# Routing searches started within the projection, first-product fill moved to later heads, one mask instruction, and both norms rearranged in a float32 block on one core

## The chip, the cores and the metric

The kernel runs on one core of a Trainium2 chip. The metric is the device time of one execution in microseconds (us). The core has TensorE (matmuls and transposes), VectorE (DVE), ScalarE (ACT), GpSimd (POOL) and SyncE (SP, which only issues transfers). Each engine works through its own instructions in a fixed order and waits on semaphores for the others.

## What is computed

One layer over 512 tokens of 1024 features, all in float32. The reference, cut to what matters:

```
xn = rms_norm(x, ln_mix_g)
proj = xn @ w_in
a_out = gmlp_spatial_gating(proj[..., :a0], proj[..., a0:a1], ...)
b_out = banded_chunk_attention(proj[..., q0:k0], proj[..., k0:v0], proj[..., v0:], ...)
x = x + concatenate([a_out, b_out]) @ w_out
x = x + peer_ffn(rms_norm(x, ln_ffn_g), w_query, sub_keys, expert_u, expert_v)
```

`rms_norm(x, g)` is `x * rsqrt(mean(x*x) + eps) * g`. `peer_ffn` routes each token: for each of 8 heads a query of two halves of 128 is projected, each half is scored against 128 sub-keys, the 16 best of each half are kept, their 256 sums are searched for the best 16 pairs, and a softmax over those gives gates to 16 of 16384 experts:

```
q = (xb @ w_query).reshape(tokens, HEADS, 2, 128)
sc = einsum('thpd,hpkd->thpk', q, sub_keys)
s_top, i_top = top_k(sc, 16)
best, pos = top_k(s_top[:, :, 0, :, None] + s_top[:, :, 1, None, :], 16)
eidx = i_top0 * 128 + i_top1 at pos
out = sum over (head, k) of softmax(best) * gelu(xb . u[eidx]) * v[eidx]
```

## The kernel before, in words

**Splitting.** Each float32 operand of a large product is split into a high and a low part, and `mm3` (lines 150 to 154) makes three matmuls of them: high x high, high x low, low x high. `load_split` (121 to 133) loads a weight tile of 128 x 1024 into `raw` (three buffers), makes `hi` on ScalarE (line 129) and `lo` on VectorE or GpSimd (line 130); `hi` and `lo` have five buffers each.

**Order.** The text order of the program and priorities give each engine its order through a scheduler, except inside a `manual_schedule` block, where the named engines keep the written order. `issue_after(i)` puts what it encloses behind instruction `i` on the engine of `i`; instructions of other engines are not bound by it.

**Opening (229 to 255).** Tokens stand in four tiles of 128. `norm_transposed` (164 to 186) takes each: ScalarE squares and sums (line 170), VectorE and ScalarE make the reciprocal root (159 to 161), VectorE multiplies by it and by the gain row, which was loaded to all partitions (173), TensorE transposes (178), ScalarE and VectorE make the high and low halves `xh` and `xl` (182, 183). Then the queries and keys are projected, token tile by token tile (253), and with the second half of their weights for all tiles (254).

**Attention and gating (282 to 442)** follow, not touched but for the row scale below.

**Second norm (455 to 478).** The output projection's residual sums (line 464) are made for token tiles in the order 1, 2, 3, 0, and each tile goes through `norm_transposed`, to `xbh` and `xbl`. `behind_norm` holds the last two instructions of tile 3, and the splits and activations of the first two expert tiles (722 to 724) and the first query weights (676) are queued behind it. These first products need tokens 128 to 447 alone, so not tile 0.

**Routing (671 to 755).** TensorE makes, head by head, the two halves of the query (685), copied to `qt` by ScalarE (688), then the scores (696), copied out by ScalarE (699, 700). VectorE finds the best 16 of each of three token tiles and two halves (`best_keys`, `top16`, 595 to 610). For the head before, `pairs` (612 to 635) makes 50 candidate sums and `choose` (637 to 658) picks 16 of them: searches, six instructions that take one bit each of the 16 positions (646), and six predicated copies down a tree of values (656). Gathers of expert rows for 64 tokens go on GpSimd (518) with their dot products on VectorE (527), six a head from head 2 on.

As the route leaves TensorE free, first products of the dense expert layer are put in between: `first_products` (584 to 591), one tile of 128 experts by 320 tokens each, split on GpSimd, activated on ScalarE (581). `FILL` gives their number per head, and eight more, the bridge, follow the last head. Lines 750 and 751 copy `xbh` and `xbl` for the later stage, on GpSimd.

**One-hot stage (850 to 914).** Gates of all experts are made from one-hot products (819) of two factors, `bm` (GpSimd, 803) and `am` (VectorE, 811), stored and reloaded; the rest of the first products run in between. **Second products (1022 to 1034)** with the values follow, TensorE without a stop, while GpSimd gathers the rows of token tile 0.

## Time and profile before

| | us |
|---|---|
| median of 3 runs | 1438.88 (1437.36 to 1449.58) |
| the profiled execution | 1439.61 |
| its span, first to last instruction | 1437.8 |
| TensorE busy | 1387.7 |
| VectorE busy | 1157.9 |
| GpSimd busy | 701.0 |
| ScalarE busy | 610.7 |

The granted TensorE clock averages 0.994 over the span. In the lines of a timeline, the first number is the start in us, the second the duration in us, then come the engine (PE, DVE, ACT, POOL, SP), the line, the operation, what it writes and reads, its shapes and the count, and in brackets how long the engine stood idle before it and what ended that. In the table of stretches come the sum of time, then each engine's busy time and its instructions, the granted clock, the transfer engines' share and GB/s. A matmul's duration overlaps its neighbour's; the distance between two starts is its price in a row of them.

### The profile page before, as it was taken

The numbers are of one execution on the slowest core, as the hardware profiler recorded it, in microseconds if no ns is written. First come the engines' busy times: TensorE is split into PE (matmuls) and PEld (weight loads), VectorE is DVE, ScalarE is ACT, GpSimd is POOL, SyncE is SP. The second block draws the span as 40 slices with busy tenths as digits, with TensorE's granted clock in tenths as the row PEclk, the third lists the DMA queues.
The fourth block names the chain that finished last, engine by engine and source line by source line (L and its number), as shares of the span: only waits on it lengthen the run. The fifth ranks groups of instructions, "written<-read, shape, count | busy, mean of one in ns | idle before, by whom it ended". The sixth has DMA issues, their size and how long they took to land.

```text
span 1437.8 us, 21717 instructions
## 1 busy us (share of the span) xinstructions
PE 1387.7 (97%) x7808; PEld 1226.3 (85%) x7808; DVE 1157.9 (81%) x2548; ACT 610.7 (42%) x974; POOL 701.0 (49%) x479
## 2 busy tenths in 40 slices
...
GB/s 190 118 189 75 89 99 195 101 272 303 214 223 206 313 327 268 282 259 350 279 361 358 332 351 355 354 385 363 396 337 355 366 325 352 276 327 348 344 327 72
DMA packets 164315, 396.77 MB, mean 276 GB/s; under 512 B 12736, under 2 KB 75088, under 8 KB 162160
## 3 DMA queue, kind: packets, MB, share of 16 engines
...
q14 instruction: 46, 0.38, 0.1%
...
## 4 chain that ended last, share of the span: by engine, by line
PE 77%; DVE 12%; DMA 5%; ACT 3%; issue 2%; POOL 1%; SPq 0%; ACTq 0%; POOLq 0%; DVEq 0%
PE pa L1008 22%; PE px L1008 11%; PE pu L152 9%; PE pu L154 9%; PE pu L153 9%; PE pa L152 4%; PE pa L153 4%; PE pa L154 4%; PE pa L819 3%; DMA gd<-gst 2%; DVE lo L130 2%; POOL bm L803 1%; DVE acc L960 1%; DVE tree L656 1%; DVE rowe L527 1%
## 5 line engine op out<-in xcount | busy, mean ns | idle before, releaser
L129 ACT ACTIVATE hi<-raw 128x1024 fp32r<-128x1024 f32 x300 | 316.7, 1059 | 447.9 <-DMA raw<-in_vd 133.1
L130 DVE TENSOR_TENSOR lo<-raw,hi 128x1024 fp32r<-128x1024 f32 x247 | 310.3, 1257 | 90.1 <-ACT hi L129 89.0
L947 POOL DMA_INDIRECT row<-in_ud,eint x128 | 196.0, 1531 | 176.0 <-DVE acc L960 109.3
L958 POOL DMA_INDIRECT row<-in_vd,eint x128 | 185.2, 1447 | 173.6 <-DVE row L949 120.2
L152 PE MATMUL pu<-xch,hi 128*128 128x320 f32 x784 | 246.8, 315 | 3.1 <-ACT act L581 3.1
L153 PE MATMUL pu<-xcl,hi 128*128 128x320 f32 x784 | 242.0, 309 | 0.0
L154 PE MATMUL pu<-xch,lo 128*128 128x320 f32 x784 | 241.6, 308 | 0.0
L1008 PE MATMUL pa<-hi,wh 128*128 128x512 f32 x512 | 199.8, 390 | 0.0
L1008 PE MATMUL pa<-lo,wh 128*128 128x512 f32 x512 | 199.3, 389 | 0.0
L960 DVE SCALAR_TENSOR_TENSOR acc<-row,hw,acc 128x1024 f32<-128x1024 f32 x128 | 164.8, 1287 | 0.9 <-DMA row<-in_vd,eint 0.5
L130 POOL TENSOR_TENSOR lo<-raw,hi 128x1024 fp32r<-128x1024 f32 x53 | 126.9, 2408 | 69.3 <-ACT hi L129 68.5
L949 DVE SCALAR_TENSOR_TENSOR row<-row,xb 128x1024 f32<-128x1024 f32 x128 | 157.4, 1232 | 1.5 <-DMA row<-in_ud,eint 1.5
L1008 PE MATMUL pa<-hi,wl 128*128 128x512 f32 x512 | 158.3, 389 | 0.0
L152 PEld LDWEIGHTS pu<-xch,hi 128*128 128x128 f32 x784 | 147.7, 188 | 6.5 <-ACT act L581 5.0
L153 PEld LDWEIGHTS pu<-xcl,hi 128*128 128x128 f32 x784 | 147.7, 188 | 1.4
L154 PEld LDWEIGHTS pu<-xch,lo 128*128 128x128 f32 x784 | 147.6, 188 | 0.0
L819 PE MATMUL pa<-bm,am 128*128 128x128 f32 x768 | 98.5, 281 | 16.7 <-DVE am L811 6.4
L1008 PEld LDWEIGHTS pa<-hi,wl 128*128 128x128 f32 x512 | 96.1, 188 | 20.4
L1008 PEld LDWEIGHTS pa<-hi,wh 128*128 128x128 f32 x512 | 96.1, 188 | 20.3
L1008 PEld LDWEIGHTS pa<-lo,wh 128*128 128x128 f32 x512 | 96.1, 188 | 20.2
L819 PEld LDWEIGHTS pa<-bm,am 128*128 128x128 f32 x768 | 92.9, 195 | 21.5 <-POOL bm L803 7.5
L1008 PE MATMUL px<-hi,wh 128*128 128x512 f32 x256 | 100.5, 393 | 3.2 <-ACT hi L129 3.2
(224 smaller groups left out, 2633.6 us busy)
## 6 DMA issues: line engine op xcount, KB each, us to landing
raw<-in_uT SPq DMA_DIRECT2D x128, 512.0 KB, 5.7
raw<-in_vd SPq DMA_DIRECT2D x128, 512.0 KB, 6.1
...
gc<-gd SPq DMA_DIRECT2D x15, 256.0 KB, 10.8
```

What stands on the lines that cost most here:

```text
L129: nc.scalar.activation(hi, raw, AF.Copy)
L130: ins = eng.tensor_tensor(lo, raw, hi.bitcast(F32), op=ALU.subtract)
L152: nc.tensor.matmul(ps, lh[0], rh[0], start=first, stop=False)
L153: nc.tensor.matmul(ps, lh[0], rh[1], start=False, stop=False)
L154: nc.tensor.matmul(ps, lh[1], rh[0], start=False, stop=last)
L527: nc.vector.scalar_tensor_tensor(row, row, 1.0, xbu, op0=ALU.mult, op1=ALU.mult, accum_out=du[:, j:j + 1])
L819: nc.tensor.matmul(ps[:, i * P:(i + 1) * P], am[:, 4 * q + i, :], bm[:, 4 * q + i, :], start=True, stop=True)
L947: nc.gpsimd.indirect_dma_start(out=row, out_offset=None, in_=ud, in_offset=bass.IndirectOffsetOnAxis(ap=eint[:, j:j + 1], axis=0))
L949: nc.vector.scalar_tensor_tensor(row, row, 1.0, xb0, op0=ALU.mult, op1=ALU.mult, accum_out=hw[:, j:j + 1])
L958: nc.gpsimd.indirect_dma_start(out=row, out_offset=None, in_=vd, in_offset=bass.IndirectOffsetOnAxis(ap=eint[:, j:j + 1], axis=0))
L960: nc.vector.scalar_tensor_tensor(acc0, row, hw[:, j:j + 1], acc0, op0=ALU.mult, op1=ALU.add)
L1008: nc.tensor.matmul(accs[t][half], (wh, wh, wl)[k][:, b, tok], w[b][k % 2][:, ds_], start=first and k == 0, stop=last and k == 2)
```

## The change

The first norm: raw x is transposed and multiplied by the gain per feature (the gain now lies on partitions, 4 KB instead of a broadcast of 512 KB), and 1/rms is put in after the products, as the scale of the copies out of PSUM; the gated part takes it as a row (`rrow`), made by four transposes. The opening's order on TensorE, VectorE, ScalarE and SyncE is written out by hand, the first weights are loaded and split in pieces, and TensorE multiplies a tile of ones (8 products ahead of the first transposes, 5 behind them).

The second norm: the second expert tile's split waits for the scaling of the last tile in order (tile 0), the activations and the first query weights for that tile's halves; GpSimd's two copies come behind its splits of head 4.

The routing: the scores of a query's first half are made in the middle of the second half's projection, those of the second half in the middle of the next head's first; the last head's come behind its first fill. `FILL` changes, with the same sum of 20. The six mask instructions become one, with a small table of bits. The gain row of the gating shares buffers with the attention's transposed weights.

```diff
-FILL = (2, 2, 2, 2, 3, 3, 3, 3)
+FILL = (0, 1, 2, 3, 4, 4, 3, 3)
 DELAY = 6
 SLACK = 4
+IDLE = (8, 5)
...
+        bits = const.tile([P, 6], U32, name="bits")
+        for i in range(6):
+            nc.gpsimd.memset(bits[:, i:i + 1], 1 << i)
...
+        roots, behind_scale, behind_norm = [], [], []
+
+        def queued_behind(marks):
+
+            ctx = ExitStack()
+            for i in marks:
+                ctx.enter_context(tc.issue_after(i))
+            return ctx
...
+        def load_pieces(src, n, b):
+
+            raw, hi, lo = big("raw", F32, RAW), big("hi", F32R, HI), big("lo", F32R, LO)
...
+            for i in range(n):
+                nc.sync.dma_start(raw[:, cs[i]] if n > 1 else raw.rearrange("p (a b) -> p a b", b=b),
+                                  src[:, i, :] if n > 1 else src)
+
+            def split(i=0):
+                nc.scalar.activation(hi[:, cs[i]], raw[:, cs[i]], AF.Copy)
+                nc.vector.tensor_tensor(lo[:, cs[i]], raw[:, cs[i]], hi[:, cs[i]].bitcast(F32), op=ALU.subtract)
...
-            nc.scalar.activation(r, r, AF.Sqrt)
+            root = nc.scalar.activation(r, r, AF.Sqrt)
+            roots[:] = [getattr(root, "ins", root)]
...
-                nc.vector.scalar_tensor_tensor(xt, tiles[t], r, gain, op0=ALU.mult, op1=ALU.mult)
+                scaled = nc.vector.scalar_tensor_tensor(xt, tiles[t], r, gain, op0=ALU.mult, op1=ALU.mult)
+                behind_scale[:] = [roots[0], getattr(scaled, "ins", scaled)]
...
-                    if t == TT - 1:
-                        behind_norm[:] = [getattr(i, "ins", i) for i in last]
+                    behind_norm[:] = [getattr(i, "ins", i) for i in last]
...
-            g1 = prea.tile([P, D], F32, name="g1")
...
+            rest0 = prea.tile([P, P], F32, name="rest0")
+            g1 = prea.tile([P, KT], F32, name="g1")
+            x_t = [prea.tile([P, D], F32, name="x_t", tag="xq", bufs=4) for t in range(TT)]
+
+            def idle_products(n):
+
+                ps = pa()
+                for _ in range(n):
+                    nc.tensor.matmul(ps[:, 0:P], rest0, rest0, start=True, stop=True)
+
+            def turned(t):
+
+                pss = [pa() for _ in range(2)]
+                for j, ps in enumerate(pss):
+                    for k in range(4):
+                        nc.tensor.transpose(ps[:, k * P:(k + 1) * P], x_t[t][:, (4 * j + k) * P:(4 * j + k + 1) * P],
+                                            ident)
+                return [ps.rearrange("p (k t) -> p k t", t=P) for ps in pss]
+
+            def gained(ps, j):
+                xg = prea.tile([P, 4, P], F32, name="xg", tag="xg", bufs=3)
+                nc.vector.tensor_tensor(xg, ps, g1[:, 4 * j:4 * j + 4, None].to_broadcast([P, 4, P]), op=ALU.mult)
+                return xg
+
+            def halves(t, j, xg):
+                to = (slice(None), slice(4 * j, 4 * j + 4), slice(t * P, (t + 1) * P))
+                return (nc.scalar.copy(xh[to], xg),
+                        nc.vector.tensor_tensor(xl[to], xg, xh[to].bitcast(F32), op=ALU.subtract))
+
+            def squares(t):
+                junk = prea.tile([P, D], BF16, name="junk", tag="junk", bufs=2)
+                nc.scalar.activation(junk, x_t[t], AF.Square, accum_out=rs1[:, t:t + 1])
+
+            def scale_of(t):
+                r = rs1[:, t:t + 1]
+                nc.vector.tensor_scalar(r, r, 1.0 / D, EPS, op0=ALU.mult, op1=ALU.add)
+                nc.scalar.activation(r, r, AF.Sqrt)
+                return nc.vector.reciprocal(r, r)
+
+            def scaled_copy(dst, ps, t):
+                return nc.scalar.activation(dst, ps, AF.Copy, scale=rs1[:, t:t + 1])
+
+            qk = [prea.tile([P, D], F32, name="qk", tag="xq", bufs=4) for t in range(TT)]
+            first = {getattr(mybir.EngineType, e) for e in ("PE", "DVE", "Activation", "SP")}
+            with tc.manual_schedule(engines=first):
+                nc.vector.memset(rest0, 1.0)
+                idle_products(IDLE[0])
+                nc.sync.dma_start(x_t[0][:, 0:512], x_r[0][:, 0:512])
+                nc.scalar.dma_start(x_t[0][:, 512:D], x_r[0][:, 512:D])
+                nc.scalar.dma_start(g1, ln1)
+                nc.scalar.activation(rest0[:, 0:1], rest0[:, 0:1], AF.Sqrt)
+                pss = turned(0)
+                squares(0)
+                idle_products(IDLE[1])
+                xg = [gained(pss[j], j) for j in range(2)]
+                halves(0, 0, xg[0])
+                w_at = Pieces(w_in, 2 * WA // CW, 2)
+                for j in range(3):
+                    w_at.load(j)
+                nc.sync.dma_start(x_t[1], x_r[1])
+                ps0 = pu()
+
+                def product(t, ps, ks):
+                    tok = slice(t * P, (t + 1) * P)
+                    for k in ks:
+                        mm3(ps, (xh[:, k, tok], xl[:, k, tok]), w_at(k), k == 0, k == KT - 1)
+
+                w_at.split(0, 0)
+                halves(0, 1, xg[1])
+                w_at.split(0, 1)
+                product(0, ps0, range(2))
+                w_at.split(1)
+                product(0, ps0, range(2, 4))
+                scale_of(0)
+                w_at.load(3)
+                w_at.split(2)
+                product(0, ps0, range(4, 6))
+                pss = turned(1)
+                w_at.split(3)
+
+                def next_halves(t, pss):
+                    xg = [gained(ps, j) for j, ps in enumerate(pss)]
+                    for j in range(2):
+                        last = halves(t, j, xg[j])
+                    squares(t)
+                    return last
+
+                next_halves(1, pss)
+                for t in range(2, TT):
+                    nc.sync.dma_start(x_t[t], x_r[t])
+                product(0, ps0, range(6, 8))
+                scaled = scale_of(1)
+                scaled_copy(qk[0][:, 0:CW], ps0, 0)
+                for t in range(1, TT):
+                    ps = pu()
+                    product(t, ps, range(6))
+                    if t + 1 < TT:
+                        last = next_halves(t + 1, turned(t + 1))
+                    product(t, ps, range(6, 8))
+                    if t + 1 < TT:
+                        scale_of(t + 1)
+                    if t < TT - 1:
+                        scaled_copy(qk[t][:, 0:CW], ps, t)
+            scaled_copy(qk[t][:, 0:CW], ps, t)
...
+            marks = [getattr(i, "ins", i) for i in last]
+            with tc.issue_after(marks[0]), tc.issue_after(marks[1]):
+                w1 = chunk_of(w_in, 2 * WA // CW + 1, CW)
+            token_major(xh, xl, w1, lambda t, ps: scaled_copy(qk[t][:, CW:2 * CW], ps, t))
...
+                rb = prea.tile([P, P], F32, name="rb", tag="rb", bufs=2)
+                nc.vector.tensor_copy(rb, rs1[:, t:t + 1].to_broadcast([P, P]))
+                nc.tensor.transpose(ps[:, t * P:(t + 1) * P], rb, ident)
+            nc.vector.tensor_copy(rrow, ps)
...
-            for i in range(6):
-                nc.vector.tensor_scalar(mask[:, i * n * TOPK:(i + 1) * n * TOPK], bpos.rearrange("p t k -> p (t k)"),
-                                        1 << i, None, op0=ALU.bitwise_and)
             mask = mask.rearrange("p (l t k) -> p l t k", t=n, k=TOPK)
+            nc.vector.tensor_tensor(mask, bpos[:, None, :, :].to_broadcast([P, 6, n, TOPK]),
+                                    bits[:, :, None, None].to_broadcast([P, 6, n, TOPK]), op=ALU.bitwise_and)
...
+        weights_q, top_pos, qts = {}, {}, {}
+
+        def projected_keys(h, p2):
+
+            if p2 == 0:
+                if h:
+                    weights_q[h] = chunk_of(wq, h, eng=nc.gpsimd)
+                else:
+                    with queued_behind(behind_norm):
+                        weights_q[h] = chunk_of(wq, h)
+            ps = pa()
+            for k in range(KT):
+                if k == KT // 2:
+                    yield
+                mm3(ps, weights_q[h](k, slice(p2 * P, (p2 + 1) * P)), (xbh[:, k, :], xbl[:, k, :]),
+                    k == 0, k == KT - 1)
+            qts[h, p2] = rq.tile([P, S], F32, name="qt", tag="qt", bufs=2)
+            nc.scalar.copy(qts[h, p2], ps)
+
+        def best_of(h, p2):
+
+            if p2 == 0:
+                skt = rq.tile([P, 2, NK], F32, name="skt", tag="skt", bufs=2)
+                nc.sync.dma_start(skt, skT[:, 2 * h:2 * h + 2, :])
+                s0 = rq.tile([P, 2, NK], F32, name="s0", tag="s0", bufs=2)
+                top_pos[h] = (*keys(rq, ND), skt, s0)
+            top, pos, skt, s0 = top_pos[h]
+            qt = qts.pop((h, p2))
+            sp = pa()
+            for t in range(TT):
+                nc.tensor.matmul(sp[:, t * P:(t + 1) * P], qt[:, t * P:(t + 1) * P],
+                                 skt[:, p2, :], start=True, stop=True)
+            sc = rq.tile([P, ND, NK], F32, name="scr", tag="scr", bufs=2)
+            nc.scalar.copy(sc, sp.rearrange("p (t n) -> p t n", n=NK)[:, GT:, :])
+            nc.scalar.copy(s0[:, p2, :], sp[:, 0:NK])
+            for t in range(ND):
+                best_keys(rq, top, pos, t, p2, sc[:, t, :])
+            if p2:
+                nc.scalar.dma_start(s0d[h], s0.rearrange("p a n -> p (a n)"))
+
         def candidates(h):
 
-            if h:
-                w = chunk_of(wq, h, eng=nc.gpsimd)
-            else:
-                with tc.issue_after(behind_norm[0]), tc.issue_after(behind_norm[1]):
-                    w = chunk_of(wq, h)
...
+                for _ in projected_keys(h, p2):
+                    if p2:
+                        best_of(h, 0)
+                    elif h:
+                        best_of(h - 1, 1)
             fill = first_products(sum(FILL[:h]) + BC, FILL[h], nc.gpsimd, True)
...
+            if h == NH - 1:
+                next(fill, None)
+                best_of(h, 1)
             for _ in fill:
                 pass
...
-        with tc.issue_after(behind_norm[0]), tc.issue_after(behind_norm[1]):
-            for _ in first_products(0, BC, nc.vector, True):
-                pass
-        cands = []
+        for j in range(BC):
+            if j >= PRE:
+                with queued_behind(behind_scale):
+                    split_tile(j, nc.vector)
+            multiply_tile(True)
+            with queued_behind(behind_norm):
+                activate_tile()
         for h in range(NH + 1):
             dots_early(0)
             if h < NH:
-                cands.append(candidates(h))
+                candidates(h)
...
-                nc.gpsimd.tensor_copy(xch, xbh[:, :, T0:T0 + NDU])
-                nc.gpsimd.tensor_copy(xcl, xbl[:, :, T0:T0 + NDU])
+                with queued_behind(splits):
+                    nc.gpsimd.tensor_copy(xch, xbh[:, :, T0:T0 + NDU])
+                    nc.gpsimd.tensor_copy(xcl, xbl[:, :, T0:T0 + NDU])
```

80 lines of the change are left out of this document (26 added, 54 removed).

## The prediction

> **What bounds the kernel now.** I read the page first, then the busy time in stretches of 10 and 20 us, then the timeline of each stretch in which TensorE falls short.
>
> ```profile
> span 1437.8 us, 21717 instructions
> ...
> PE 77%; DVE 12%; DMA 5%; ACT 3%; issue 2%; POOL 1%; SPq 0%; ACTq 0%; POOLq 0%; DVEq 0%
> ```
>
> The chain that ended last runs through TensorE for 77% of the span. A change that removes no TensorE work can therefore earn only the time in which TensorE waits or runs slowly. The edits touch three such places: the opening, the second norm (220 to 229 us), and the routing with the bridge and the start of the one-hot stage (229 to 460 us). The last is the largest; the columns are TensorE, its weight loads, VectorE, ScalarE, GpSimd.
>
> ```profile
> 420.00:440.00 20.00, 16.20 (x100) 15.93 (x99) 19.52 (x70) 8.12 (x12) 13.86 (x12) 0.91 0.65 220
> 440.00:460.00 20.00, 15.00 (x105) 14.50 (x104) 19.37 (x24) 4.38 (x7) 13.71 (x10) 0.95 0.50 152
> ```
>
> VectorE is full (19.4 and 19.5 of 20) and TensorE is not: here routing is bound by VectorE's top-16 searches, choices and dot products.
>
> **Opening.** First the timeline of before.
>
> ```profile
> 4.79 1.06 ACT L170 ACTIVATE junk<-x_t 128x1024 bf16<-128x1024 f32 x1 [2.10 <-DMA x_t<-in_x]
> ...
> 13.14 0.63 PE L153 MATMUL pu<-lo,xh 128*128 128x512 f32 x1
> ...
> 13.57 0.63 PE L154 MATMUL pu<-hi,xl 128*128 128x512 f32 x1
> ...
> 14.61 0.40 PE L154 MATMUL pu<-hi,xl 128*128 128x512 f32 x1
> ...
> 14.85 0.39 PE L152 MATMUL pu<-hi,xh 128*128 128x512 f32 x1
> ...
> 19.55 0.50 PE L152 MATMUL pu<-hi,xh 128*128 128x512 f32 x1 [0.24 <-ACT xh L182]
> 19.58 1.28 DVE L183 TENSOR_TENSOR xl<-pa,xh 128x512 fp32r<-128x512 f32 x2
> ...
> 20.12 1.04 PE L178 MATMUL pa<-ident,xs 128*128 128x128 f32 x8
> ...
> 20.91 0.47 PE L154 MATMUL pu<-hi,xl 128*128 128x512 f32 x1
> ...
> 21.55 1.23 DVE L130 TENSOR_TENSOR lo<-raw,hi 128x1024 fp32r<-128x1024 f32 x1 [0.62 <-ACT hi L129]
> ```
>
> x lands at 4.79. Token tile 1 starts its products at 19.55, and from 20.91 TensorE no longer stops. By then it has two products (0.23 each, the start-to-start at 14.61 and 14.85) and eight transposes (0.9) beyond tile 0's work, so the unbroken stretch "begins" at 19.5. The change multiplies by the gain alone after transposing the raw x, and puts the row scale into the copies out of PSUM; square, root and reciprocal leave the path. VectorE then sets it, in an order written by hand: two gains and two low halves of tile 0 (4 x 0.64, half of the x2 row at 19.58), two half splits (2 x 0.64), three whole ones (3 x 1.23), the scale (0.3), then two gains and the first low half of tile 1 (3 x 0.64): 9.7 us. They start when the first transposes are out, about 5.4, which makes 15.1 without a wait. I add 2.2: 0.3 for ScalarE's square ahead of the first copy, 0.9 because the root of tile 0 stands on ScalarE between the second and third split, 0.6 for the fourth weight piece (its load waits for a raw buffer), 0.4 for hand-overs. Tile 1 at 17.3: 2.2 won. Four more transposes (the row of scales) cost 4 x 0.13 of TensorE (the x8 row at 20.12): **-1.7 us**. The bounds are -4 (no wait) and +1 (one load of weights late by a transfer). The pre-run products on a constant tile lie in idle TensorE time. The removed 512 KB of broadcast gains and the scaled copies (ScalarE, TensorE not waiting on them) cost or earn nothing more.
>
> The clock belongs to this row: 13.14 to 13.57 is 0.43 per product, 14.61 to 14.85 is 0.24. The Trainium skill (TensorE: Matmul & The Clock Gate, What's actually happening) says that the array runs at half clock until it has been busy for some 3.4 us; the trace agrees with the half. By that rule the pre-run saves at most the seven slow products of before, 7 x 0.2 = 1.4 us, which lies inside the 2.2; its Part 4 adds that transposes do not count as activity; if the gate closed again, the sum would be 1422.6.
>
> **Second norm.**
>
> ```profile
> 215.87 2.33 POOL L750 CAST xch<-xbh 128x2560 fp32r<-128x2560 f32 x1 [23.26 <-ACT xbh L182]
> ...
> 216.57 0.30 PE L152 MATMUL pu<-xbh,hi 128*128 128x320 f32 x1
> ...
> 216.80 2.48 DVE L130 TENSOR_TENSOR lo<-raw,hi 128x1024 fp32r<-128x1024 f32 x1 [0.16 <-ACT hi L129]
> ...
> 219.20 0.67 DVE L464 TENSOR_TENSOR x<-ugT,pu 128x512 f32<-128x512 f32 x1
> ...
> 219.80 3.88 DVE L130 TENSOR_TENSOR lo<-raw,hi 128x1024 fp32r<-128x1024 f32 x2
> ...
> 223.60 0.14 DVE L159 TENSOR_SCALAR rstd<-ss 128x1 f32<-128x1 f32 x1
> ...
> 225.64 1.67 PE L178 MATMUL pa<-ident,xs 128*128 128x128 f32 x8 [2.89 <-DVE xs L173]
> ...
> 228.98 0.57 PE L152 MATMUL pa<-xbh,hi 128*128 128x512 f32 x1
> ```
>
> Splits stand ahead of the last tile's norm on VectorE: the residual sum of tile 0 could run at 216.95 and runs at 219.20 (2.2 late), and L159 could run at 221.1, when the square is done, and runs at 223.60 (2.5 late). GpSimd's two casts stretch these splits from 1.23 to 2.48 and 1.94. The change queues the splits behind the norm and moves the casts to head 4. Then the transposes can go 4.7 earlier, at 221.0; but the second first-product tile now waits: its low half runs behind the scaling, 221.0 to 222.3, and its 24 products (3.5 us) end at 225.8, where the projection starts instead of at 228.98: **-3.2 us**. The bounds are 0 (another split slips in) and -4.4 (pure work of 48 small products and 8 transposes is 8.0 of the 12.4 between 216.57 and 228.98).
>
> **Routing, bridge, first one-hots.**
>
> ```profile
> 245.46 0.49 DVE L597 MAX8 top<-scr 128x8 f32<-128x128 f32 x2 [16.80 <-ACT scr L699]
> ...
> 248.87 0.39 PE L152 MATMUL pa<-xbh,hi 128*128 128x512 f32 x1
> ...
> 252.55 0.29 DVE L601 FIND_INDEX8 pos<-top,rep 128x8 uint32<-128x128 f32 x1
> ...
> 259.78 0.30 PE L152 MATMUL pu<-xbh,hi 128*128 128x320 f32 x1
> ...
> 263.30 1.95 PE L696 MATMUL pa<-skt,qt 128*128 128x128 f32 x16
> 265.00 0.39 PE L152 MATMUL pu<-xbh,hi 128*128 128x320 f32 x1
> ...
> 271.75 0.25 DVE L632 TENSOR_TENSOR cand<-top,pa 128x96 f32<-128x96 f32 x1
> ...
> 275.85 1.44 DVE L646 TENSOR_SCALAR pa<-bpos 128x48 uint32<-128x48 uint32 x6
> ...
> 281.65 0.24 DVE L658 COPY eidx<-tree 128x48 f32<-128x48 f32 x1
> ...
> 368.70 1.51 ACT L639 COPY tree<-cand 128x1536 f32<-128x1536 f32 x1
> ...
> 392.92 1.51 ACT L639 COPY tree<-cand 128x1536 f32<-128x1536 f32 x1 [8.21 <-DVE cand L632]
> ...
> 436.77 0.23 DVE L658 COPY eidx<-tree 128x48 f32<-128x48 f32 x1
> ...
> 451.88 2.05 PE L819 MATMUL pa<-bm,am 128*128 128x128 f32 x16 [0.22 <-POOL bm L803]
> ...
> 452.30 6.02 DVE L130 TENSOR_TENSOR lo<-raw,hi 128x1024 fp32r<-128x1024 f32 x1 [0.56 <-ACT hi L129]
> ...
> 459.60 2.69 PE L819 MATMUL pa<-bm,am 128*128 128x128 f32 x11 [4.78 <-DVE am L811]
> ```
>
> TensorE's pieces: both halves of a projection 10.9 (248.87 to 259.78), a fill tile 3.5 (259.78 to 263.30), a head's scores 1.7 (263.30 to 265.00). From the first projection (228.98) to the first one-hot product (451.88) stand 8 x 12.6 and 30 tiles (20 fills, 8 of the bridge, 2 behind it): 101 + 105.5 = 206.5 us. It took 222.9, so 16.4 are lost. FILL sums to 20 before and after; no product is added.
>
> VectorE's pieces: a head's searches 7.3 (245.46 to 252.84), a choice 10.1 (271.75 to 281.89), of which the six masks are 1.44. In late heads with six dot products it turns once in 24.2 (368.70 to 392.92), against 23.2 of TensorE with three fills and 19.7 with two. Before, it idles 16.8 ahead of the first search and falls behind later.
>
> One mask instruction over 288 elements: not in this trace. Bounds from its rows: 0.4 alone (a third of the 1.23 of 1024 elements), and 2.8 if it first waits out a GpSimd split. I take 0.4, so 1.0 saved per head, since nothing shows such a wait for small instructions.
>
> After: heads last 12.6, 16.1, 19.7, 23.2, 26.7, 26.7, 23.2, 23.2 by their fills 0, 1, 2, 3, 4, 4, 3, 3. The first search can start 8.2 + 1 into head 0 instead of 16.5. Head 3 starts at 48.4 after the first projection; from there VectorE needs 23.2 a head and keeps up until head 7, which starts at 148.2. There it has three half searches (the last one is no longer a head late) and the tree copy that VectorE makes itself there (1.7): 23.2 + 3.6 + 1.7 = 28.5, to 176.7. The last choice (10.8) and six dot products (6 x 1.22, from the group below) follow: choice done between 187 and 195. Before, it was done at 436.77 - 228.98 = 207.8, and the first one-hot product came 15.1 later. The same 15.1 gives 202 to 210 now, and TensorE's own work 206.5: the two meet. I take 211.4, with 3.5 for VectorE's late end and 1.4 for ScalarE's queue: **-11.5 us**. Bounds: 0, and -16.4. Scores half a projection later also take TensorE off ScalarE's copies: nothing to add, it is in the 16.4.
>
> What is moved: the two GpSimd casts (5.7 as above) come behind head 4's splits and ahead of head 5's.
>
> ```profile
> L130 POOL TENSOR_TENSOR lo<-raw,hi 128x1024 fp32r<-128x1024 f32 x29 | 69.3, 2410 | 6.7 <-ACT hi L129 6.1
> ...
> L527 DVE SCALAR_TENSOR_TENSOR rowe<-rowe,px 128x1024 f32<-128x1024 f32 x33 | 40.2, 1219 | 7.2 <-DMA rowe<-in_ud,eui 7.1
> L518 POOL DMA_INDIRECT rowe<-in_ud,eui x35 | 33.5, 956 | 10.1 <-issue 8.9 <-DVE gate L600 0.3 <-PE pu L154 0.3
> ```
>
> Head 4 then asks GpSimd for six splits (14.5), six gathers with their gaps (6 x 1.2) and the casts: 27.4 against TensorE's 26.7. Split tiles made ahead (five buffers) cover 0.7 us; without that lead it costs those 0.7.
>
> After 451.88 one more stall follows, 4.8 behind a VectorE split of 6.02. With VectorE less behind I take **-2** (bounds 0 and -4.8). The rest of the one-hot stage and the second product I leave as they are.
>
> **Sum.** The profiled execution took 1439.6 (span 1437.8 and 1.8 around it), the median is 1438.9. 1439.6 - 1.7 - 3.2 - 11.5 - 2.0 = **1421.2**; the likeliest case runs from 1415 to 1428.
>
> **Rivals.**
> (a) *VectorE stays the bound because the mask waits.* It now has two SBUF inputs. The row for: 216.80, a two-input split that took 2.48 beside a GpSimd cast. If each mask waits one GpSimd split (2.4), a head gets 1.4 dearer instead of 1.0 cheaper; five heads and the last choice lose 6 x 2.4 = 14.4, the choice ends at 201 to 209, products at 217 to 224: routing earns some 2, the stall after it stays. 1439.6 - 1.7 - 3.2 - 2 = 1432.7. Against: GpSimd splits for 69 of 140 us, so half the masks meet none. The Trainium skill (SBUF - State Buffer, Who interferes with whom) states this as an exclusive lock for a VectorE instruction with two SBUF inputs against a GpSimd one that reads SBUF; the rows of 2.48 and 6.02 agree.
> (b) *GpSimd's supply decides.* Raw weights have three buffers; each burst of three splits then waits for a load. With some 5 us of such waiting in heads 3 to 7 and the bridge beyond its lead, routing keeps 4 of its 11.5 and the stall stays: 1439.6 - 4.9 - 4 = 1430.7. Against: only 6.7 of idle stands before those splits from 300 to 440.
> (c) *Slower: ScalarE is held by the late half.* The searches of a head's second half now end inside the next head, and the casts and tree copy that wait for them (the 8.21 at 392.92) stand on ScalarE ahead of the next query copy and the evacuations. It decides once VectorE is more than 2.7 (half of one half's projection) late: 8.2 - 2.7 = 5.5 in each of heads 2 to 7 is 33 in place of the 16.4 lost now: 1439.6 - 4.9 + 16.6 = 1451.
> (d) *More:* with no backlog TensorE's shortfalls of the one-hot stage shrink too, by some 6: 1415.
>
> **Chances.** Forecast 0.52, (a) 0.12, (b) 0.16, (c) 0.06, (d) 0.14. A measurement of this kernel tells about 1%, 14.4 us, from no change: faster means below 1424.5. That is three quarters of the forecast's own range, all of (d) and little of (a) and (b): 0.56. Slower is (c), 0.06; the rest 0.38. The range reaches to (d) and past (a) and (b): 1411 to 1434; (c) is left out.
>
> **What would show it.** Opening: the second tile's first product near 17 us. Norm: the first projection about 5 us earlier, near 224, and no split between the last residual and its scaling. Routing: first search 9 us after the first projection, query-copy waits gone, first one-hot product near 435 (451.88 before), VectorE idle before head 3 and no longer full to 440. Mask rows of 0.4 confirm the price, rows of 2 mean (a); long GpSimd idle before splits means (b); ScalarE waiting on candidates while TensorE waits on query copies means (c). An unchanged first one-hot product would make the forecast wrong.

## The result and the profile after

The changed kernel takes 1453.47 us (median) where the kernel before took 1443.4 us beside it: the ratio is 1.0061, 95% interval 1.0043 to 1.0079 (one of its eleven runs, 2158.38 us at a granted clock of 0.592, is left out of the ratio). It is slower by 0.6%, where 1.2% faster was forecast. The profiled execution took 1449.6 us (span 1447.8, before 1437.8), 28.4 above the forecast 1421.2. Stretch by stretch, from the timelines:

| stretch | before | forecast | after |
|---|---|---|---|
| start to the first projection of a query | 228.98 | 224.1 | 223.59 |
| from there to the first one-hot product ("the stretch" below) | 222.9 | 211.4 | 236.1 |
| from there to the first second product | 155.8 | 153.8 | 156.4 |
| from there to the end of the span | 830.1 | 830.1 | 831.7 |

The rows of after behind the table, from its timeline: the second tile's first product, the last scaling and its transposes, the first projection, the first search, the end of the last choice, the first one-hot product, and the first second product.

```profile
16.80 0.47 PE L192 MATMUL pu<-hi,xh 128*128 128x512 f32 x1
...
217.79 1.28 DVE L214 SCALAR_TENSOR_TENSOR xs<-x,rstd,g2row 128x1024 f32<-128x1024 f32 x1
...
219.22 1.06 PE L220 MATMUL pa<-ident,xs 128*128 128x128 f32 x8
...
223.59 0.39 PE L192 MATMUL pa<-xbh,hi 128*128 128x512 f32 x1
...
233.44 0.49 DVE L732 MAX8 top<-scr 128x8 f32<-128x128 f32 x2 [9.12 <-ACT scr L838]
...
440.64 0.24 DVE L792 COPY eidx<-tree 128x48 f32<-128x48 f32 x1
...
459.70 2.05 PE L975 MATMUL pa<-bm,am 128*128 128x128 f32 x16 [1.86 <-POOL bm L959]
...
616.10 0.79 PE L1164 MATMUL px<-hi,wh 128*128 128x512 f32 x1 [3.32 <-ACT hi L154]
```

and the last of these of before:

```profile
607.69 0.50 PE L1008 MATMUL px<-hi,wh 128*128 128x512 f32 x1 [3.25 <-ACT hi L129]
```

Up to 233 all went as forecast. Then the stretch, which should have shrunk by 11.5, grew by 13.2. Its row in the profile's table of stretches, before and after:

```profile
228.98:451.88 222.90, 212.73 (x1249) 195.88 (x1248) 181.58 (x844) 90.52 (x155) 154.33 (x104) 0.99 0.65 221
...
223.59:459.70 236.11, 215.28 (x1251) 197.85 (x1249) 195.87 (x806) 93.15 (x157) 161.58 (x107) 0.97 0.62 211
```

With almost the same count of instructions, TensorE (first busy time) is busy 2.6 longer and idle 20.8 instead of 10.2. The waits of the stretch (totals of 223 to 460; the columns are the sum, the times and the longest), before:

```profile
ACT top L624 <- DVE pos L601: 20.8, 5, 6.7
...
DVE rowe L527 <- DMA rowe<-in_ud,eui: 7.1, 10, 2.3
PE pu L152 <- ACT act L581: 6.7, 2, 3.8
```

and after:

```profile
ACT top L759 <- DVE pos L736: 28.3, 6, 9.0
...
DVE rowe L662 <- DMA rowe<-in_ud,eui: 17.9, 12, 5.6
...
PE pu L192 <- ACT act L716: 14.6, 4, 7.3
```

Three waits that belong together are longer: VectorE for gathered rows, ScalarE for positions that VectorE's searches give, TensorE for an accumulator that ScalarE has not evacuated. One stall of after, followed back in its timeline:

```profile
354.69 7.37 POOL L155 TENSOR_TENSOR lo<-raw,hi 128x1024 fp32r<-128x1024 f32 x3
...
365.31 2.41 POOL L155 TENSOR_TENSOR lo<-raw,hi 128x1024 fp32r<-128x1024 f32 x1 [0.17 <-ACT hi L154]
...
368.70 1.01 POOL L653 DMA_INDIRECT rowe<-in_ud,eui  x1 [0.27 <-POOL eui L669]
...
370.09 0.28 DVE L734 MATCH_REPLACE8 rep<-top,scr 128x128 f32<-128x128 f32 x1
...
375.94 1.22 DVE L662 SCALAR_TENSOR_TENSOR rowe<-rowe,px 128x1024 f32<-128x1024 f32 x1 [5.57 <-DMA rowe<-in_ud,eui]
...
378.49 0.29 DVE L736 FIND_INDEX8 pos<-top,rep 128x8 uint32<-128x128 f32 x1
...
378.81 0.23 ACT L759 CAST top<-pos 128x48 f32<-128x48 uint32 x1 [9.04 <-DVE pos L736]
...
379.11 0.31 PE L194 MATMUL pu<-xbh,lo 128*128 128x320 f32 x1
...
383.93 1.50 ACT L774 COPY tree<-cand 128x1536 f32<-128x1536 f32 x1 [2.79 <-DVE cand L767]
...
386.30 0.41 ACT L716 ACTIVATE act<-pu 128x320 f32<-128x320 f32 x1
...
386.76 0.64 PE L192 MATMUL pu<-xbh,hi 128*128 128x320 f32 x1 [7.35 <-ACT act L716]
```

Read it upward from TensorE. It waits 7.35 for the activation at 386.30. ScalarE comes to it only after the work that had piled up, and after 2.79 more in front of the tree copy at 383.93, which needs VectorE's candidates. Before that it had stood 9.04 in front of the cast at 378.81, which needs the last positions of a late half. VectorE gave those only at 378.49, since its order puts dot products (375.94) into the middle of that half's searches, and the first of them waited 5.57 for a gather. GpSimd issued that gather at 368.70, behind its splits, and it landed 7.2 later. Each engine keeps its order; the lateness is handed from one to the next.

The stall costs more than its length: the product at 386.76 takes 0.64 us against 0.31 at 379.11, the twelve products from 386.76 to 389.86 take 3.1 us where the last twelve before the stall took 1.8, and the granted clock of the window (third number from the end) is 0.83:

```profile
360.00:380.00 20.00, 19.41 (x111) 17.32 (x109) 14.29 (x44) 5.92 (x13) 15.70 (x12) 1.00 0.83 276
380.00:400.00 20.00, 13.24 (x64) 11.96 (x65) 18.87 (x90) 7.81 (x12) 12.17 (x8) 0.83 0.48 155
```

VectorE (third busy time) was no longer full before the stall, 14.29 of 20, and TensorE lost time all the same. The idle time won on VectorE ahead of the first search (9.12 in place of 16.80) was lost again in waits for rows (17.9 in place of 7.1).

The mask is the other surprise (groups of VectorE, 220 to 470; after the bar busy time and mean ns):

```profile
L781 DVE TENSOR_TENSOR pa<-bpos,bits 128x288 uint32<-128x288 uint32 x8 | 14.4, 1803 | 0.2
```

One mask instruction takes 1.80 on the mean, against 0.4 forecast and 1.25 for the six (10.0 in eight heads). One of the eight ran at 0.46, the other seven at 1.45 to 2.28.

### The profile page after: what moved, and what is told of

Its sections match the earlier page's. It is cut to its first block, busy times and chain, and to the rows that moved or that the text cites. A ratio compares the mean times of both kernels' runs of the same rounds, so it can differ in the third digit from the quotient of the medians.

```text
span 1447.8 us, 21693 instructions
## 1 busy us (share of the span) xinstructions
PE 1398.1 (97%) x7838; PEld 1234.6 (85%) x7838; DVE 1167.1 (81%) x2478; ACT 613.0 (42%) x975; POOL 700.7 (48%) x485
## 4 chain that ended last, share of the span: by engine, by line
PE 70%; DVE 14%; DMA 7%; POOL 3%; issue 3%; ACT 2%; ACTq 0%; POOLq 0%; SPq 0%; DVEq 0%
PE pa L1164 21%; PE px L1164 11%; PE pu L194 8%; PE pu L192 8%; PE pu L193 8%; PE pa L192 3%; PE pa L194 3%; PE pa L193 3%; PE pa L975 3%; DVE lo L155 2%; DMA rowe<-in_ud,eui 2%; DMA gd<-gst 2%; DVE row L1105 2%; DVE rowe L662 2%; POOL lo L155 1%
## 5 line engine op out<-in xcount | busy, mean ns | idle before, releaser
L154 ACT ACTIVATE hi<-raw 128x1024 fp32r<-128x1024 f32 x296 | 312.7, 1058 | 451.1 <-DMA raw<-in_vd 136.3
L155 DVE TENSOR_TENSOR lo<-raw,hi 128x1024 fp32r<-128x1024 f32 x243 | 301.7, 1243 | 77.8 <-ACT hi L154 77.2
L1103 POOL DMA_INDIRECT row<-in_ud,eint x128 | 201.7, 1576 | 192.9 <-DVE acc L1116 128.6
L1114 POOL DMA_INDIRECT row<-in_vd,eint x128 | 180.5, 1410 | 164.6 <-DVE row L1105 109.5
L1164 PEld LDWEIGHTS pa<-hi,wh 128*128 128x128 f32 x512 | 96.4, 188 | 20.8
L1164 PEld LDWEIGHTS pa<-lo,wh 128*128 128x128 f32 x512 | 96.4, 188 | 20.4
```

The lines of the kernel that those rows point to most:

```text
L154: nc.scalar.activation(hi, raw, AF.Copy)
L155: ins = eng.tensor_tensor(lo, raw, hi.bitcast(F32), op=ALU.subtract)
L1103: nc.gpsimd.indirect_dma_start(out=row, out_offset=None, in_=ud, in_offset=bass.IndirectOffsetOnAxis(ap=eint[:, j:j + 1], axis=0))
L1114: nc.gpsimd.indirect_dma_start(out=row, out_offset=None, in_=vd, in_offset=bass.IndirectOffsetOnAxis(ap=eint[:, j:j + 1], axis=0))
L1164: nc.tensor.matmul(accs[t][half], (wh, wh, wl)[k][:, b, tok], w[b][k % 2][:, ds_], start=first and k == 0, stop=last and k == 2)
```

## The experiments

Theory B: ScalarE, in order, is the link that hands VectorE's lateness to TensorE. Theory G, its companion: what makes VectorE late is the gathers. The rivals: S, GpSimd's supply of splits; V, the sum of VectorE's work; M, the mask; K and K', the moved casts; O, the order that the scheduler writes, which any edit changes. All measurements in one table (the ratio is to the kernel before on the same chip, over all runs; stretch and waits are of one profiled execution, waits as totals of 223 to 460; - means none listed):

| kernel | ratio (95%) | stretch | VectorE for rows | ScalarE for positions | TensorE for activations |
|---|---|---|---|---|---|
| before | 1 | 222.9 | 7.1 | 20.8 | 6.7 |
| after | 1.0061 (1.0043-1.0079) | 236.1 | 17.9 | 28.3 | 14.6 |
| old_routing | 1.0039 (1.0021-1.0058) | 233.1 | 13.1 | 17.5 | 13.5 |
| casts_vec | 1.0029 (1.0003-1.0055) | 231.9 | 18.8 | - | 12.2 |
| late_dots | 1.0061 (1.0040-1.0082) | 235.5 | 16.3 | 27.4 | 13.2 |
| still_dots | 0.9944 (0.9923-0.9965) | 219.8 | - | 11.7 | 3.5 |
| front_six | 0.9995 (0.9970-1.0020) | 225.4 | 8.2 | 14.2 | 6.5 |
| six_masks | 1.0037 (1.0015-1.0059) | 236.6 | 21.2 | 26.1 | 15.1 |
| dots_cand | 1.0133 (1.0088-1.0177) | 246.9 | - | 27.8 | 19.4 |
| dots_cand_six | 1.0054 (1.0034-1.0074) | 235.1 | - | 18.4 | 9.8 |
| casts_tree_vec | 0.9995 (0.9976-1.0014) | 225.1 | 5.6 | - | - |
| ctv_free | 1.0117 (1.0076-1.0158) | 247.9 | 20.4 | - | 12.3 |
| ctv_front | 1.0036 (1.0017-1.0056) | 235.4 | 4.0 | - | 6.2 |
| ctv_sbuf | 1.0218 (1.0193-1.0244) | 255.5 | 8.1 | - | 18.1 |
| ctv_six | 0.9981 (0.9965-0.9998) | 227.5 | 6.7 | - | 2.9 |
| front_oldcast | 0.9940 (0.9917-0.9964) | 224.5 | 6.2 | 20.7 | 8.9 |
| after_oldcast | 1.0065 (1.0043-1.0087) | 235.0 | 13.7 | 22.0 | 6.5 |
| ctv_six_oldcast | 0.9994 (0.9974-1.0013) | 226.0 | 6.0 | - | 0.5 |
| front_oldcast_mask | 1.0015 (0.9994-1.0037) | 232.8 | 10.9 | 22.6 | 14.4 |
| order_alone | 1.0146 (1.0107-1.0186) | 244.4 | 29.2 | 32.0 | 21.9 |

### Is it the routing, and through which link?

`old_routing`: after, with `candidates` of before; the rest of the change stays.

```
-FILL = (0, 1, 2, 3, 4, 4, 3, 3)
+FILL = (2, 2, 2, 2, 3, 3, 3, 3)
...
-                for _ in projected_keys(h, p2):
-                    if p2:
-                        best_of(h, 0)
-                    elif h:
-                        best_of(h - 1, 1)
+                for k in range(KT):
+                    mm3(ps, w(k, slice(p2 * P, (p2 + 1) * P)), (xbh[:, k, :], xbl[:, k, :]),
+                        k == 0, k == KT - 1)
```

> The changed kernel with the routing's order and the fill of before (both halves projected, a fill tile, both scores; 2,2,2,2,3,3,3,3 fill tiles); the new opening, the new second norm, the one mask instruction and the moved casts stay. Theory B (ScalarE, in order, is blocked by casts and tree copies that wait for the late half's searches, and TensorE waits for ScalarE's evacuations): the block belongs to the new order, so the stretch from the first projection to the first one-hot product goes from 236.1 back to 222 or, with the cheaper masks, to 215-222; time 1430 to 1436, that is 5 to 10 below the kernel before in the same call. Rival S (the loss sits in GpSimd's supply of split weights, with the casts moved into head 4): the stretch stays above 228. Rival L (what opening and norm win is lost later whatever the routing does): the time is that of the kernel before.

Measured: 233.1, so theory B's forecast missed and the new order can't be all of it; mask or casts do harm in the old routing as well. VectorE's waits for rows and TensorE's for activations are there too, ScalarE's for positions are below those of before. TensorE's longest wait, 9.3 at 414.45, isn't theory B's: the split ahead of the activation on ScalarE stood for raw weights.

```profile
413.02 1.06 ACT L154 ACTIVATE hi<-raw 128x1024 fp32r<-128x1024 f32 x1 [14.07 <-DMA raw<-in_uT]
```

That is a lack of supply, so rival S is alive in the old order; `front_oldcast_mask` below shows the same chain.

`casts_vec`: the three small operations ahead of the candidates on VectorE in every head.

```
-                    cand = pairs(rq, *top_pos.pop(h - 1)[:2], ND, ps[:, 6 * ND * TOPK:8 * ND * TOPK], h >= NH - 1)
+                    cand = pairs(rq, *top_pos.pop(h - 1)[:2], ND, ps[:, 6 * ND * TOPK:8 * ND * TOPK], True)
```

> The changed kernel, with the three small operations ahead of the candidates (copy of the best values, scaled cast, cast of the positions) on VectorE in every head instead of on ScalarE; the tree copy stays on ScalarE. Theory B: ScalarE is no longer held by positions that VectorE has not found; TensorE's waits on first-product evacuations (14.6 in all) shrink to under 5, the stretch of 236.1 shrinks to 222-230, time 6 to 13 less than the changed kernel; VectorE gets some 0.6 a head more. Rival S (supply of splits by GpSimd): no difference, the waits on low halves stay. Rival V (VectorE's sum of work alone sets the stretch): 0 to 5 slower than the changed kernel.

Measured: 231.9, 4 better, and TensorE's waits still 12.2. The timeline of this kernel shows why:

```profile
370.20 1.22 DVE L662 SCALAR_TENSOR_TENSOR rowe<-rowe,px 128x1024 f32<-128x1024 f32 x1 [5.26 <-DMA rowe<-in_ud,eui]
...
379.59 1.49 ACT L774 COPY tree<-cand 128x1536 f32<-128x1536 f32 x1 [9.95 <-DVE cand L767]
...
382.41 0.63 PE L192 MATMUL pu<-xbh,hi 128*128 128x320 f32 x1 [7.13 <-ACT act L716]
```

The wait went over to the next instruction of ScalarE that needs VectorE, the tree copy. So that was moved as well:

```
-                           nc.vector.tensor_copy if h >= NH - 1 else nc.scalar.copy)
+                           nc.vector.tensor_copy)
```

> The changed kernel with everything on ScalarE that waits for VectorE's searches and candidates (three small operations and the tree copy of each head) on VectorE instead. VectorE gets some 0.9 + 1.75 more work in each of six heads, 16 in all; the gathers and the places of the dot products stay late. Theory B (ScalarE, in order, is the link that carries VectorE's waits to TensorE): ScalarE no longer waits for positions or candidates, TensorE's waits for the evacuation of first-product tiles (14.6) fall under 3, the stretch of 236.1 falls to 222-230 and the time 6 to 13 below the changed kernel, although VectorE does more and still waits for gathers. Rival V (the sum of VectorE's work and waits sets the stretch by itself): the stretch grows to 240 or more.

Measured (`casts_tree_vec`): 225.1, ratio 0.9995. Its waits list has no line of TensorE for activations at all; TensorE's longest single wait, and VectorE's waits for rows:

```profile
DVE rowe L662 <- DMA rowe<-in_ud,eui: 5.6, 4, 3.3
...
PE pa L835 <- issue: 3.9, 1, 3.9
```

Theory B holds: VectorE was given some 16 us more work, and 11.0 of the stretch came back. Rival V falls for this order. VectorE's own waits shrank too, for rows by 12.3, for scores (which ScalarE copies out) behind the first search from 10.8 to 3.3: ScalarE, once held, had held VectorE in turn. The forecast that VectorE would still wait for gathers as before missed, so the run doesn't tell what made VectorE late at first.

### What makes VectorE late?

`still_dots`: the dot products of routing and bridge read a constant tile, so the gathered rows are left out of the result.

```
+                row = still.pop() if still else row
                 nc.vector.scalar_tensor_tensor(row, row, 1.0, xbu, op0=ALU.mult, op1=ALU.mult,
                                                accum_out=du[:, j:j + 1])
+                if row is kept[0]:
+                    still.append(row)
```

> The changed kernel, in which the dot products of routing and bridge read a constant tile in place of the gathered rows (the early half of the expert dot products is left out of the result); the gathers are still issued, the dot products are as many and as large, only none waits for a gather. Theory B with late gathers: VectorE's waits for rows (17.9) are gone, the stretch of 236.1 falls to 222-228, time 8 to 13 less than the changed kernel. If ScalarE's block comes from VectorE's sum of work (rival V), 0 to 4 less. Rival S (supply): within 2.

Measured: 219.8 and 0.9944, 1.2% below after, more than expected, with the casts still on ScalarE; the block all but closes (TensorE 3.5). It looks like theory G, but the edit did more than take the waits away. The dot products of this kernel and of after, from 220 to 460 (count, shortest, median and longest ns, first and last start):

```profile
L666 DVE SCALAR_TENSOR_TENSOR still<-still,px x42: 1194/1210/1229, 228.4 to 351.3; 128x1024 f32<-128x1024 f32 x42
...
L662 DVE SCALAR_TENSOR_TENSOR rowe<-rowe,px x42: 1182/1211/1223, 269.3 to 455.5; 128x1024 f32<-128x1024 f32 x42
```

As they need no gather, the scheduler placed all 42 early, the first ahead of the first search, and none between the searches of the late heads. So three things are gone at once from the late heads: the wait for rows, the dot products between the searches, and VectorE's work on the 18 dot products (22 us) that after runs from 352 to its last choice. The run shows that the loss hangs on the dot products in the late heads; which of the three does it, it can't tell.

`late_dots` was to do this without leaving work out:

```
         for h in range(NH + 1):
-            dots_early(0)
             if h < NH:
                 candidates(h)
+                dots_early(0)
```

> The changed kernel, with the dot products of the gathered rows placed behind a head's projections, searches and fill in the program instead of ahead of them. Theory B with the ingredient that gathers land late and the dot products, waiting in the middle of the searches, hold VectorE: its 17.9 of waits for gathered rows fall under 6, ScalarE's waits for positions (28.3) fall under 18, time 6 to 13 less than the changed kernel. Rival V (VectorE's sum of work) and rival S (supply): within 2 of the changed kernel.

Nothing changed. The scheduler put the dot products into the same places between the searches, so this run tells nothing about the theories. `dots_cand` forced them, behind the last candidate sum (`paired`) of the same head.

```
-                nc.vector.scalar_tensor_tensor(row, row, 1.0, xbu, op0=ALU.mult, op1=ALU.mult,
-                                               accum_out=du[:, j:j + 1])
+                with queued_behind(paired):
+                    nc.vector.scalar_tensor_tensor(row, row, 1.0, xbu, op0=ALU.mult, op1=ALU.mult,
+                                                   accum_out=du[:, j:j + 1])
```

> The changed kernel with the dot products of the gathered rows queued behind the candidates of the same head on VectorE, so that none stands between the searches up to head 7. Theory G: VectorE's waits for gathered rows (17.9) fall under 6, ScalarE's waits for positions (28.3) under 18, the stretch of 236.1 comes to 220-226 as with the constant tile (219.8), time 10 to 16 less than the changed kernel, that is 1436 to 1443. Rival V (the sum of VectorE's work sets the stretch): within 3 of the changed kernel, since no work is removed.

Measured: no wait for rows, and yet 246.9. The waits of this kernel:

```profile
DVE top L733 <- ACT scr L840: 31.6, 10, 9.3
ACT top L760 <- DVE pos L737: 27.8, 6, 10.5
...
PE pu L192 <- ACT act L717: 19.4, 6, 7.9
```

The expectation missed. Six dot products now stand together ahead of the choice, and positions are late without any wait for a gather: VectorE waits for scores from ScalarE, ScalarE for positions from VectorE. And the mask got dearer (groups of VectorE, 220 to 475):

```profile
L783 DVE TENSOR_TENSOR pa<-bpos,bits 128x288 uint32<-128x288 uint32 x8 | 26.4, 3300 | 0.5
```

That is 12.0 more than in after; three of the eight took 6.56 to 6.57, each beside three splits in a row on GpSimd. The block needs late positions, whatever makes them late.

`dots_cand_six` has the six masks of before in it as well (the diff stands at `six_masks`):

> The kernel with the dot products behind the candidates, and six mask instructions instead of the one. Theory G alone: as the kernel with the dot products behind the candidates, within 2. Theory M beside it: 2 to 5 less than that.

Measured: 235.1, 11.8 less than `dots_cand`, more than either theory had: the six masks take 10.0 where the one had come to 26.4. Beside `six_masks` below, which has the dot products between the searches and the same masks, the waits for rows fall from 21.2 to none and TensorE's for activations from 15.1 to 9.8, but the stretch only from 236.6 to 235.1, and the ratios overlap. This pair gives theory G no support: taking the waits for rows away in this manner won nothing that can be told from noise.

`ctv_free` is `casts_tree_vec` with the gathers let go from behind the splits:

```
-                with tc.issue_after(splits[0]):
-                    indices_early(h - 2)
-                    ready_early(h - 2)
-                    gather_early(EARLY, gat, ROWA)
+                indices_early(h - 2)
+                ready_early(h - 2)
+                gather_early(EARLY, gat, ROWA)
```

> The kernel with ScalarE freed of the waits, and also without the rule that a head's gathers are issued behind its last split on GpSimd. Theory G (gathers issued late, so VectorE stands): the gathers are issued among the splits, VectorE's waits for gathered rows fall under 8, the stretch is 3 to 8 shorter than with ScalarE freed alone, time to match. Rival S (GpSimd's supply): low halves come later, TensorE waits for them, 0 to 6 slower than with ScalarE freed alone.

Measured: 247.9. Rows were waited for longer (20.4), and ScalarE waited 58.0 for raw weights (32.6 in `casts_tree_vec`): the splits now stand among the gathers on GpSimd. Rival S, and dearer than it had said.

### The parts by themselves

`front_six`: opening, second norm and moved casts alone (`old_routing` with the six masks).

> The new opening and the new second norm with the moved casts alone: routing order, fill and six mask instructions of before. Theory M (the one mask instruction loses: it has run 1.2 to 1.8 us where the six together took 1.25, and it shifts the dot products that stood between the six masks): the stretch from the first projection to the first one-hot product returns from 233.1 to 221-224, time 4 to 6 below the kernel before. Rival K (the casts in head 4, behind its splits, are what costs the old routing 10): the stretch stays at 230 or more and the time is at or above that of before.

Measured: 225.4, between the two forecasts, and a time that can't be told from before. `front_oldcast` also leaves the two casts free, as before.

```
-                with queued_behind(splits):
-                    nc.gpsimd.tensor_copy(xch, xbh[:, :, T0:T0 + NDU])
-                    nc.gpsimd.tensor_copy(xcl, xbl[:, :, T0:T0 + NDU])
+                nc.gpsimd.tensor_copy(xch, xbh[:, :, T0:T0 + NDU])
+                nc.gpsimd.tensor_copy(xcl, xbl[:, :, T0:T0 + NDU])
```

> The new opening and second norm with everything of before behind it: order, fill, six masks, and the casts free to run early again. Theory K' (the moved casts give back what opening and norm win: with them the stretch was 225.4 against 222.9, and the time that of before): the casts run in the second norm or ahead of head 4, the stretch is 222-224, time 3 to 5 below before. Rival O (the routing loop of VectorE, ScalarE and GpSimd turns any shift of its start into another sum of waits): the stretch lands anywhere from 219 to 230, and the gain of 5 isn't seen whole.

Measured: 0.9940 in four runs, the lowest ratio of all, faster than both kernels. Where its casts run (timeline, GpSimd):

```profile
214.71 2.33 POOL L890 CAST xch<-xbh 128x2560 fp32r<-128x2560 f32 x1 [23.27 <-ACT xbh L224]
216.98 2.32 POOL L891 CAST xcl<-xbl 128x2560 fp32r<-128x2560 f32 x1
```

and in `front_six`:

```profile
309.43 2.32 POOL L891 CAST xch<-xbh 128x2560 fp32r<-128x2560 f32 x1
...
321.71 2.33 POOL L892 CAST xcl<-xbl 128x2560 fp32r<-128x2560 f32 x1
```

In the second norm they make the first projection 0.8 later (224.90 against 224.13); in the routing they cost 0.55% of the whole. In the profiles 0.9 of it lies in the stretch (225.4 - 224.5) and 5.0 between it and the second products (159.3 against 154.3); why there isn't settled. The two ratios come from different chips, and their intervals are only just apart.

`front_oldcast_mask`: `front_oldcast` with the one mask instruction of the change.

> The kernel with the new opening and second norm and everything else of before, but with the one mask instruction. It tells the mask by itself: the one instruction ran 0.45 alone and 2 to 4.6 beside a GpSimd split. Theory M (it loses, and so does the order that it brings: dot products no longer stand between the six masks): 0.3 to 0.6% slower than with the six (0.994), that is 0.997 to 1.000 of before. Forecast of the prediction (saves 1.0 a head where VectorE is the bound): 0.990 to 0.994.

Measured: 1.0015 where the six masks had 0.9940; the intervals stand apart. In this old order the one instruction, with the order that the scheduler then writes, costs 0.75%, 10.8 us. (The profiled execution, 1454.62, is the slowest of this kernel's ten.) First its own time, in this kernel's timeline:

```profile
272.33 0.47 DVE L781 TENSOR_TENSOR pa<-bpos,bits 128x288 uint32<-128x288 uint32 x1
...
296.19 7.11 POOL L155 TENSOR_TENSOR lo<-raw,hi 128x1024 fp32r<-128x1024 f32 x3
296.32 1.20 DVE L662 SCALAR_TENSOR_TENSOR rowe<-rowe,px 128x1024 f32<-128x1024 f32 x1
...
297.45 6.18 DVE L781 TENSOR_TENSOR pa<-bpos,bits 128x288 uint32<-128x288 uint32 x1
```

Then a chain later on that took 10.73 from TensorE:

```profile
398.72 0.95 POOL L653 DMA_INDIRECT rowe<-in_ud,eui  x1 [0.31 <-issue]
...
404.92 0.19 POOL L669 CAST eui<-eidx 64x8 int32<-64x8 f32 x1 [3.24 <-DMA rowe<-in_ud,eui]
...
409.16 6.96 POOL L155 TENSOR_TENSOR lo<-raw,hi 128x1024 fp32r<-128x1024 f32 x3
...
415.95 1.06 ACT L154 ACTIVATE hi<-raw 128x1024 fp32r<-128x1024 f32 x1 [13.90 <-DMA raw<-in_uT]
...
417.38 0.64 PE L192 MATMUL pu<-xbh,hi 128*128 128x320 f32 x1 [10.73 <-ACT act L716]
```

In this order GpSimd's cast of the next head's indices comes between gathers and waits for those in flight; the splits behind it, and with them the raw buffers and their loads, are late. The eight mask instructions together take 11.5, only 1.5 more than the 10.0 of the six; so most of the 10.8 is the order and what the long one delays, which this run doesn't separate.

`six_masks` is after with the six masks:

```
-            nc.vector.tensor_tensor(mask, bpos[:, None, :, :].to_broadcast([P, 6, n, TOPK]),
-                                    bits[:, :, None, None].to_broadcast([P, 6, n, TOPK]), op=ALU.bitwise_and)
+            for i in range(6):
+                nc.vector.tensor_scalar(mask[:, i * n * TOPK:(i + 1) * n * TOPK], bpos.rearrange("p t k -> p (t k)"),
+                                        1 << i, None, op0=ALU.bitwise_and)
```

> The changed kernel with the six mask instructions of before in place of the one. Theory M: 4 less VectorE time (14.4 against 10.0), and the stretch of 236.1 falls by 4 to 8. Theory G (VectorE, in its fixed order, stands for gathered rows in the middle of the late half's searches; ScalarE waits for the positions, TensorE for ScalarE): the dot products still stand between the late half's searches of heads 6 and 7 in VectorE's order, so the waits for gathered rows stay above 12 and the stretch above 231.

Measured: 236.6, rows 21.2, as theory G said. The ratio's interval (1.0015 to 1.0059) overlaps that of after, so the mask's part there isn't settled: theory M's 4 to 8 did not come. With ScalarE freed as in `casts_tree_vec`, `ctv_six` puts the six masks in:

> The kernel with ScalarE freed of casts and tree copies, and with six mask instructions instead of the one. Theory M (the one mask instruction, with both inputs in SBUF, waits for GpSimd and so costs more than the six): VectorE's masks go from 9.5 to 10.0 in all here, so no difference by durations; a difference above 4 either way would be the order that the planner writes (rival O).

Measured: 227.5 against 225.1, and ratios that overlap: no difference above 4, as expected.

`after_oldcast`, the casts alone left free in the changed kernel (the diff of `front_oldcast`):

> The changed kernel, with the two big GpSimd casts left free as before (the planner puts them into the second norm again) in place of head 4. Theory K' (the moved casts hold GpSimd for 4.6 in the head that asks most of it; with the old routing that was worth 0.5% of the whole): the wait of 2.7 for a low half behind them goes, time 5 to 8 below the changed kernel, the first projection 1 to 3 later. Theory B alone (ScalarE's block in the new order): the waits of TensorE on ScalarE stay at 10 or more, so no more than 3 below the changed kernel.

Measured: 1.0065. The wait of 2.7 for a low half is gone and the stretch is 1.1 shorter, but the first projection is 1.7 later (225.27); in the new order the casts' place decides nothing. Theory B held: the column shows 6.5 of TensorE for activations, but TensorE waited 5.5 more for ScalarE, behind a tree copy, a split and a query copy, 12.0 in all.

`order_alone`: `front_oldcast` with `candidates` of the change, so the new order with old fill, six masks and free casts.

> The kernel with the new opening and second norm and everything else of before (0.994 of before), with the new order of projections, scores and searches alone: old fill (2,2,2,2,3,3,3,3), six masks, casts left free. Theory F (the fill of 4 in heads 4 and 5 overloads GpSimd, the order itself is harmless): 0.990 to 0.995 of before. Theory B (the order lets late-half positions hold ScalarE): dot products still stand between the late half's searches, ScalarE's waits for positions stay above 20, and the time is 0.998 to 1.006 of before.

Measured: 1.0146, 2.1% above `front_oldcast`: the direction of theory B, and dearer than its range. Its waits (223 to 470):

```profile
ACT top L759 <- DVE pos L736: 32.0, 6, 11.6
DVE rowe L662 <- DMA rowe<-in_ud,eui: 29.2, 14, 5.3
...
PE pu L192 <- ACT act L716: 21.9, 5, 8.6
```

The order by itself is what loses most; the later fill that came with it wins part of that back (`six_masks`, which has it, is at 1.0037; the casts also differ, which `after_oldcast` shows to be nothing in this order).

### Do the repairs add?

`ctv_six_oldcast`: ScalarE freed, six masks and free casts in one.

> The changed kernel with all three suspected costs taken out: ScalarE freed of casts and tree copies, six masks, casts left free in the second norm. If the three add (theory B 0.66%, the casts 0.5%, the masks 0.15%), the time is 0.990 to 0.994 of before, that is 1430 to 1435 beside a before of 1444. If the loop only turns shifts into other waits (rival O), it is 0.996 to 1.002.

Measured: 0.9994. They don't add. `ctv_front`: `front_six` with ScalarE freed.

> The kernel with the new opening and second norm alone (order, fill and six masks of before), with ScalarE freed of the casts and tree copies as well. Theory B: its own block (waits of first products 6.5, of query copies 3.4) goes, the stretch from the first projection to the first one-hot product falls from 225.4 to 214-222, time 0.2 to 0.7% below the kernel before. Rival V: VectorE's 16 more make the stretch 228 to 240 and the time 0.2 to 0.8% longer than before.

Measured: 1.0036, against 0.9995 without it, the numbers of rival V. That VectorE's extra work is all of it isn't shown: TensorE's longest wait, 9.6 for a query copy, stands behind a ScalarE that waited 14.2 for raw query weights. `ctv_sbuf`: `casts_tree_vec` with masks and first values in SBUF.

```
-                ps = pa()
-                mask = ps[:, 0:6 * ND * TOPK].bitcast(U32)
+                mask = rq.tile([P, 6 * ND * TOPK], U32, name="mask", tag="mask", bufs=1)
+                pair = rq.tile([P, 2 * ND * TOPK], F32, name="pair", tag="pair", bufs=1)
```

> The kernel with ScalarE freed of casts and tree copies, with the masks and the first candidates' values in SBUF instead of in one of the four PSUM buffers that projections and scores share. Theory P (what is left of the loss after ScalarE is freed is PSUM: TensorE's scores waited 3.9 at 389.9 for a buffer that the choice held, and the clock was low after it): that wait goes, the stretch falls from 225.1 to 219-222, time 3 to 6 below the kernel with ScalarE freed. Rival O (the order that the planner then writes decides, and it moves parts of the choice behind the next searches): the stretch stays within 3 or grows, as dot products and gathers come later.

Measured: 1.0218 and 255.5. The scheduler now puts parts of the choice behind the next searches; this is rival O, and whether PSUM holds what is left of the stretch stays open.

## Why the prediction was wrong

- **Opening: right.** 17.3 forecast, 16.80 measured, 19.55 before.
- **Second norm: right.** Opening and norm together 4.9 forecast, 5.4 measured at the first projection. Alone they give 0.6% (`front_oldcast`), some 9 us; its profile shows 4.1 of it at the first projection, and where the rest lies isn't shown.
- **Routing: wrong, and this is the step:** "VectorE needs 23.2 a head and keeps up until head 7", so that the choice is done "between 187 and 195", with "1.4 for ScalarE's queue". The first search did start 9.9 after the first projection (16.5 before), and the query-copy waits (3.1 before) did go. But the last choice was done 217.3 after the first projection, where 208.0 had been the time before. From the first search to there VectorE took 207.4 in place of 191.5: it was busy 9.7 longer, 4.4 of it in the masks that should have saved 8 (the rest isn't traced), and waited 28.7 in place of 22.5, 17.9 of it for rows. The 23.2 is work without these waits, and they fell in the middle of searches that ScalarE's next instruction needed. The first one-hot product then came 18.8 later, not 15.1.

  On TensorE's side 4.9 was to be lost beyond the 206.5 of its own work; it stood idle for 20.8 (14.6 for activations, 2.7 for a low half behind the moved casts, 3.6 at the softmax and the first one-hot; 10.2 in all before). The 206.5 itself is reached in no run: TensorE is busy 215.3 here and was 212.7 before. By the starts in the timelines, products further apart than in an unbroken row (0.147 and 0.227), like those at 386.76, make some 9 of it here and some 6 before, an estimate.
- **The right case was on the list, as (c), with 0.06.** Its block, ScalarE held by the late half, is what the runs show, and its price, 16.6 more, is near the 13.2 measured. The nearness is in part luck: it reckoned a loss for TensorE of 5.5 in each of six heads, and TensorE's waits for activations are 14.6, 7.9 more than before. Two things were missing: that an engine may be late by waits and not by work, so that "VectorE no longer full" is no sign of safety; and that the dot products, which before stood between the masks, would come between the searches of late heads. The condition given, 2.7 late, was met by one gather (5.57). That ScalarE is the link, `casts_tree_vec` shows, and that the new order loses, `order_alone` against `front_oldcast`. What makes VectorE late in that order stays open: the gathers do it in the stall followed above, but `dots_cand_six` has no wait for rows and isn't faster than `six_masks`.
- **Mask: the wrong end of its bounds.** 0.4 to 2.8 was the range, 0.4 was taken "since nothing shows such a wait for small instructions"; the mean is 1.80. Rival (a) had the mechanism, and the rule of the Trainium skill that it cited (SBUF - State Buffer, Who interferes with whom) agrees with the rows of 6.18 and 1.20: the dot product with one input in PSUM isn't stretched beside the same splits.
- **Moved casts: too small in one order.** 0.7 forecast; 0.55% (8 us) in the old order, nothing that can be told from noise in the new.
- **The stall after the stretch: gone, and replaced.** The 4.8 behind a VectorE split went, a wait of 3.3 for `bm` came; from the first one-hot to the first second product it is 156.4, not 153.8.
